# A ring of its own for the modulation weights, and another start: x first, constants off SyncE, first pieces of 2, 2, 4 and 8 row chunks

## The chip, the cores and the metric

The kernel runs on one core of one Trainium2 chip. The metric is the device time of one execution in microseconds (us). The engines named here are TensorE (PE; its weight loads are PEld), VectorE (DVE), ScalarE (ACT), GpSimd (POOL) and SyncE (SP), which in this kernel issues the loads of the large weights. PEclk is the share of full speed that TensorE's clock was granted.

## What is computed

One step of a transformer of two layers, width 2048, for 128 prompt tokens and 128 sample tokens. The two sets are called groups here. Each group has a conditioning vector (`c_ctx` for the prompt, `c` for the sample), from which every layer makes six vectors of 2048 (the modulation: shift1, scale1, gate1, shift2, scale2, gate2):

```python
mod_ctx = silu_ctx @ w_mod[l] + b_mod[l]
mod_lat = (silu_c @ w_mod[l] + b_mod[l])[:, None, :]
h = rmsnorm(x, norm1) * (1.0 + scale1) + shift1
proj = h @ w_in
mix = jnp.concatenate([attn_out, o_gla], axis=-1) @ w_out
x = x + gate1 * mix
h2 = rmsnorm(x, norm2) * (1.0 + scale2) + shift2
x = x + gate2 * (jnp.square(jax.nn.relu(h2 @ w_up)) @ w_down)
```

Between `proj` and `mix` stand softmax attention (8 heads, 2 of keys and values) and a gated linear attention (GLA) in two directions. All weights are float32. `w_mod` has 2048 x 12288 entries a layer, 201 MB for both layers; in all 613 MB are moved.

## The kernel before

**Products.** Each large product is cut into blocks of 512 output columns (`block`, L303). A block goes over its 2048 rows in chunks of 256 rows: SyncE loads a chunk (tile `raw`, 512 KB, L320, in a ring of eight buffers), ScalarE casts it (L107, `wh`) and VectorE subtracts (L108, `wl`), so that the weights stand in a high and a low part. The normed and transposed x stands in a high and a low part as well (`TH`, `TL`). For each chunk, group and half, TensorE makes three products: L345 (xh wh), L346 (xl wh) and L347 (xh wl). These are called products below; there are 8640 of them, counted from 1 in the order in which TensorE runs them. In layer 0, 1 to 432 are the first half of the rows of the input projection (nine blocks), 433 to 864 the second half, 865 to 1248 the output projection, 1249 to 4320 the MLP. Layer 1 has 4321 to 5184 (input projection), 5185 to 5568 (output projection), and the MLP.

**Modulation.** `w_mod` is loaded in tiles of 512 KB (`rawm`), as a rule 128 rows by 1024 columns. On TensorE (`mod_pe`, L210 to L224) a tile gives two float32 products of 32 rows by 512 columns (L219; the trace has two records for each) into a quarter of the tile `mod`; L195 and L197 then turn the sums. `mod_first` (L226 to L254) does the same for shift1 and scale1 of layer 0, in four quarters of their columns (L237), 16 tiles each. Some segments are summed on VectorE beside the MLP instead (`mod_dve`, L264 and L270). The modulation on TensorE is a generator that the blocks pump: `N_MOD` (L34) says how many tiles go with a block of each phase, `BATCH` that they go in fours, and `need` pumps until a named segment is done. The tiles come from the same ring as the weight chunks:

```python
raw = rawp.tile([P, 1024], F32, tag="raw", name="rawm")
nc.sync.dma_start(raw, I["w_mod"][l, kc * P:(kc + 1) * P, c0:c0 + 1024])
```

**Start.** SyncE loads the identity (L91), the conditioning vectors (L133, L134), rows of biases and norm weights (L153 to L158), and the first modulation tiles (L233); GpSimd loads x. x is normed without the modulation and transposed (`xT0`, L104). When a quarter of shift1 and scale1 is there, `modulate` makes the quarter of TH and TL, and after each of the first two quarters the nine blocks of the projection run over these two chunks. The sums wait in tiles `part`.

**Norms.** At a norm the second group lags behind the first by `LAG` chunks (L41). The first group's rows go over VectorE (`xn`, L368) to TensorE's transposes (`xnT`, L104), ScalarE and VectorE (`xv`, L379 and L381) to TH and TL.

**What sets the order.** The order on each engine is made by the tile framework with a simulated timeline, and each engine then runs its instructions in that order. A load stands in SyncE's queue until its buffer is free, and every load behind it waits as well.

## Time and profile before

| | |
|---|---|
| time of three executions | 2413.31, 2416.92, 2418.26 us (median 2416.92) |
| the profiled execution: span | 2416.7 us |
| TensorE busy | 2352.2 us, 97% |
| VectorE, ScalarE, GpSimd busy | 1635.4, 1090.3, 192.0 us |
| moved by DMA | 613.20 MB, 254 GB/s in the mean |
| granted TensorE clock, mean | 0.990 |

The first instruction and the last bound the span; the median of the times is 0.2 us longer. A busy time is the sum of an engine's instructions without overlap. In a list of waits the time is that in which the engine stood still in front of an instruction, put down to what came last. In a timeline each row is one or more like instructions in a row, with the time from the first start to the last end.

### The profile page before, as it was taken

The numbers are of one execution on the slowest core, as the hardware profiler recorded it, in microseconds if no ns is written. First come the engines' busy times: TensorE is split into PE (matmuls) and PEld (weight loads), VectorE is DVE, ScalarE is ACT, GpSimd is POOL, SyncE is SP. The second block draws the span as 40 slices with busy tenths as digits, with TensorE's granted clock in tenths as the row PEclk, the third lists the DMA queues.
The fourth block names the chain that finished last, engine by engine and source line by source line (L and its number), as shares of the span: only waits on it lengthen the run. The fifth ranks groups of instructions, "written<-read, shape, count | busy, mean of one in ns | idle before, by whom it ended". The sixth has DMA issues, their size and how long they took to land.

```text
span 2416.7 us, 32872 instructions
## 1 busy us (share of the span) xinstructions
PE 2352.2 (97%) x12533; PEld 1778.1 (74%) x12533; DVE 1635.4 (68%) x1936; ACT 1090.3 (45%) x1470; POOL 192.0 (8%) x253
## 2 busy tenths in 40 slices
PE   6999999989999999999999999999999999999998
PEld 2655555767878878878876767777788888888887
...
GB/s 299 270 335 332 288 277 281 284 290 191 297 301 310 303 278 309 296 184 296 302 273 256 184 233 230 245 263 263 227 287 279 190 177 202 189 183 191 193 179 182
DMA packets 274334, 613.20 MB, mean 254 GB/s; under 512 B 24273, under 2 KB 24785, under 8 KB 274177
## 3 DMA queue, kind: packets, MB, share of 16 engines
...
HBM read 601.01 MB, written 10.03 MB: 253 GB/s over the span
## 4 chain that ended last, share of the span: by engine, by line
PE 86%; DVE 4%; DMA 4%; issue 3%; POOL 1%; ACT 1%; SPq 0%; POOLq 0%; DVEq 0%; ACTq 0%
PE acc L345 25%; PE acc L347 25%; PE acc L346 25%; PE mod L219 4%; PE mod L237 2%; DVE wl L108 1%; DMA rawm<-in_w_mod_dram 1%; DMA raw<-in_w_up_dram 1%; PE aT L104 1%; DMA raw<-in_w_down_dram 1%; DVE ga L270 1%; DMA rows<-in_b_mod_dram 1%; PE sc L577 1%; PE mod L277 1%; PE xnT L104 1%
## 5 line engine op out<-in xcount | busy, mean ns | idle before, releaser
L108 DVE TENSOR_TENSOR wl<-raw,wh 128x1024 fp32r<-128x1024 f32 (+1 forms) x586 | 692.1, 1189 | 423.6 <-ACT wh L107 407.4
L107 ACT CAST wh<-raw 128x1024 fp32r<-128x1024 f32 (+1 forms) x586 | 592.4, 1017 | 785.1 <-PE acc L346 623.8
L345 PE MATMUL acc<-wh,TH 128*128 128x512 f32 x2248 | 892.8, 398 | 1.1 <-ACT wh L107 1.0
L346 PE MATMUL acc<-wh,TL 128*128 128x512 f32 x2248 | 882.5, 393 | 0.4 <-DVE TL L108 0.4
L347 PE MATMUL acc<-wl,TH 128*128 128x512 f32 x2248 | 862.4, 396 | 1.6 <-DVE wl L108 1.6
L345 PEld LDWEIGHTS acc<-wh,TH 128*128 128x128 f32 x2248 | 423.7, 189 | 139.5 <-issue 27.3
L347 PEld LDWEIGHTS acc<-wl,TH 128*128 128x128 f32 x2248 | 422.8, 189 | 126.4 <-issue 16.6
L346 PEld LDWEIGHTS acc<-wh,TL 128*128 128x128 f32 x2248 | 423.9, 189 | 94.0 <-issue 6.8
L270 DVE SCALAR_TENSOR_TENSOR ga<-rawm,CT,ga 128x1024 f32<-128x1024 f32 x300 | 378.1, 1278 | 28.8 <-DMA rawm<-in_w_mod_dram 27.7
L108 DVE TENSOR_TENSOR wx<-raw,wx 128x1024 fp32r<-128x1024 f32 (+1 forms) x182 | 194.5, 1079 | 102.8 <-ACT wx L107 102.7
L107 ACT CAST wx<-raw 128x1024 fp32r<-128x1024 f32 (+1 forms) x182 | 168.0, 937 | 192.6 <-PE acc L346 146.2
L345 PE MATMUL acc<-wx,TH 128*128 128x512 f32 x632 | 247.6, 392 | 0.0
L346 PE MATMUL acc<-wx,TL 128*128 128x512 f32 x632 | 246.9, 391 | 0.0
L347 PE MATMUL acc<-wx,TH 128*128 128x512 f32 x632 | 239.6, 390 | 0.0
L345 PEld LDWEIGHTS acc<-wx,TH 128*128 128x128 f32 x632 | 119.5, 189 | 25.9 <-issue 0.8
L346 PEld LDWEIGHTS acc<-wx,TL 128*128 128x128 f32 x632 | 119.4, 189 | 25.1
L347 PEld LDWEIGHTS acc<-wx,TH 128*128 128x128 f32 x632 | 119.2, 189 | 25.1
L219 PE MATMUL mod<-rawm,CT 128*32 128x512 f32 x640 | 115.8, 610 | 4.4 <-DMA rawm<-in_w_mod_dram 2.5
L237 PE MATMUL mod<-rawm,CT 128*32 128x512 f32 x256 | 58.2, 653 | 18.9 <-DMA rawm<-in_w_mod_dram 18.9
...
L219 PEld LDWEIGHTS mod<-rawm,CT 128*32 128x32 f32 x640 | 18.9, 109 | 45.0 <-issue 40.0
L812 ACT ACTIVATE relu<-acc 128x512 f32<-128x512 f32 x64 | 37.9, 592 | 30.4 <-PE acc L347 30.4
(242 smaller groups left out, 1343.2 us busy)
## 6 DMA issues: line engine op xcount, KB each, us to landing
...
raw<-in_w_up_dram SPq DMA_DIRECT2D x256, 512.0 KB, 4.6
raw<-in_w_down_dram SPq DMA_DIRECT2D x256, 512.0 KB, 5.3
...
```

Of the source, the lines that this page charges most:

```text
L104: nc.tensor.transpose(dst[:, j], s, ident)
L107: nc.scalar.copy(hi, v)
L108: nc.vector.tensor_tensor(out=lo, in0=v, in1=hi.bitcast(F32), op=ALU.subtract)
L219: nc.tensor.matmul(ps[32 * q:32 * q + 32, :], CT[:, 2 * kc:2 * kc + 32], raw[:, cc * 512:(cc + 1) * 512], start=kc == 0, stop=kc == KC - 1)
L237: nc.tensor.matmul(ps[r:r + 32, :], CT[:, 4 * ch + 2 * k:4 * ch + 2 * k + 32], raw[:, k], start=ch == 0, stop=ch == KC // 2 - 1)
L270: nc.vector.scalar_tensor_tensor(out=ga[g], in0=raw, scalar=c, in1=ga[g], op0=ALU.mult, op1=ALU.add)
L277: nc.tensor.matmul(ps[32 * q:32 * q + 32, :], unit[:, 1 - g:33 - g], acc[q // 2][g][:, (q % 2) * 512:(q % 2) * 512 + 512], start=g == 0, s ...
L345: nc.tensor.matmul(acc[g], xh, wh[:, k, :], start=first, stop=False)
L346: nc.tensor.matmul(acc[g], xl, wh[:, k, :], start=False, stop=False)
L347: nc.tensor.matmul(acc[g], xh, wl[:, k, :], start=False, stop=final)
L577: nc.tensor.matmul(sps[hh][w_ * c:w_ * c + w_, n], EB[r, n % 4, j0:j0 + w_], EA[r, n % 4, i0:i0 + w_], start=True, stop=True, tile_positio ...
L812: nc.scalar.activation(r, acc, AF.Relu)
```

## The change

- The modulation tiles on TensorE no longer come from the ring of the weight chunks, but by `mod_raw` from a ring that `in_turn` sets: in the first phase four slices of a buffer of tag TH and the tiles QT, KT, BF and BB; from each layer's start on eight slices of a TH and a TL buffer; from the second half of the Q columns on the ring of the weight chunks again (`shared`); and before the output projection eight slices of a TH and a TL buffer.
- x is loaded first, on SyncE; the identity and the conditioning vectors on ScalarE's queue; the rows of biases and norm weights on GpSimd's.
- shift1 and scale1 come in pieces of 2, 2, 4, 4 and 4 row chunks of 128 columns each (`FIRST`, then 8 to 12 and 12 to 16). The first two have tiles of 128 x 4 x 256 in place of 128 x 2 x 512. The nine blocks of the first phase run three times, over 1, 1 and 2 chunks of 256 rows, where they ran twice over 2.
- `N_MOD` has other numbers, and two of them a phase for the projections; the second norm's segments are asked for in the last block of the output projection and not before it.

```diff
-N_MOD = dict(a=(2, 4), b=9.25, out0=4, c=6, out1=3)
...
+N_MOD = dict(a=(0.9, 1.8, 3.6), b=(9, 5), out0=7.75, c=(7, 4), out1=4)
+FIRST = ((0, 2), (2, 4), (4, 8))
...
-        nc.sync.dma_start(ident, I["ident"])
+        nc.scalar.dma_start(ident, I["ident"])
...
+        rowt = big("PM", (P, 8, P), "rowt")
...
+        nc.scalar.dma_start(crow[0:16], I["c_ctx"].rearrange("(k p) -> k p", p=P))
+        nc.scalar.dma_start(crow[16:32], I["c"].rearrange("o (k p) -> (o k) p", p=P))
+        x0 = []
+        for g, n in enumerate(("x_prompt", "x_sample")):
+            x0.append([big("E", name="x0") for _ in range(2)])
+            for h in range(2):
+                nc.sync.dma_start(x0[g][h], I[n][0][:, h * 1024:(h + 1) * 1024])
...
-            nc.sync.dma_start(rows[0:96], I["b_mod"][l].rearrange("(k p) -> k p", p=P))
-            nc.sync.dma_start(rows[96:112], I["norm1"][l].rearrange("(k p) -> k p", p=P))
...
+            load(rows[0:96], I["b_mod"][l].rearrange("(k p) -> k p", p=P))
+            load(rows[96:112], I["norm1"][l].rearrange("(k p) -> k p", p=P))
...
-        def mod_turn(ps):
+        def mod_turn(ps, n=4):
...
-            for h in range(2):
+            for h in range(n // 2):
...
+        ring, turn = [], [0]
+        def in_turn(*parts):
+            ring[:] = [p for ps in zip(*parts) for p in ps] if len(parts) > 1 else parts[0]
+            turn[0] = 0
+        def bank(tag):
+            t = tp.tile([P, 4, 1024], F32, tag=tag, name="bank")
+            return [lambda j=j: t[:, j] for j in range(4)]
+        def mod_raw():
+            make = ring[turn[0] % len(ring)]
+            turn[0] += 1
+            return make()
+        shared = [lambda: rawp.tile([P, 1024], F32, tag="raw", name="rawm")]
...
                 for half in range(2):
-                    raw = rawp.tile([P, 1024], F32, tag="raw", name="rawm")
+                    raw = mod_raw()
...
-        def mod_first(l, q):
+        def mod_first(l, k0, nk):
             ps = ps_mod.tile([P, 512], F32, tag="mod", name="mod")
-            for ch in range(KC // 2):
+            n, per = nk * P, 8 // nk
+            for ch in range(KC // per):
                 for a in range(2):
-                    raw = rawp.tile([P, 2, 512], F32, tag="raw", name="rawm")
-                    c0 = a * D + q * 512
-                    nc.sync.dma_start(raw, I["w_mod"][l, ch * 256:(ch + 1) * 256, c0:c0 + 512]
+                    raw = mod_raw().rearrange("p (c n) -> p c n", n=n)
+                    c0 = a * D + k0 * P
+                    nc.sync.dma_start(raw, I["w_mod"][l, ch * per * P:(ch + 1) * per * P, c0:c0 + n]
                                       .rearrange("(c p) n -> p c n", p=P))
-                    for k in range(2):
-                        r = 32 * (a * 2 + k)
-                        nc.tensor.matmul(ps[r:r + 32, :], CT[:, 4 * ch + 2 * k:4 * ch + 2 * k + 32], raw[:, k],
-                                         start=ch == 0, stop=ch == KC // 2 - 1)
-                    if ch < KC // 2 - 1 or a < 1:
+                    for k in range(per):
+                        kc = ch * per + k
+                        r = 32 * (a * 2 + k % 2)
+                        nc.tensor.matmul(ps[r:r + 32, 0:n], CT[:, 2 * kc:2 * kc + 32], raw[:, k],
+                                         start=kc < 2, stop=kc >= KC - 2)
+                    if ch < KC // per - 1 or a < 1:
                         yield
-            pt = mod_turn(ps)
...
-        on_pe = mods([(mod_first, 0, q) for q in range(4)]
+        on_pe = mods([(mod_first, 0, k0, k1 - k0) for k0, k1 in FIRST + ((8, 12), (12, 16))]
...
-            tiles = [big("E", name="x0") for _ in range(2)]
-            for h in range(2):
-                load(tiles[h], x_in[g][:, h * 1024:(h + 1) * 1024])
             ss = stile(4, "ss")
-            xt = [tiles[q // 2][:, (q % 2) * 512:(q % 2) * 512 + 512] for q in range(4)]
+            xt = [x0[g][q // 2][:, (q % 2) * 512:(q % 2) * 512 + 512] for q in range(4)]
...
+        in_turn(bank("TH"), [lambda t=t: big(t, name="rawm") for t in ("QT", "KT", "BF", "BB")])
...
-        for q in range(4):
-            need(0, "first", q)
+        def first(k0, k1):
+            need(0, "first", k0)
             for g in range(2):
-                modulate(0, 0, g, q, xT0[:, 4 * q:4 * q + 4, g * P:(g + 1) * P], TH, TL)
-            if q > 1:
-                continue
+                modulate(0, 0, g, k0, k1 - k0, xT0[:, k0:k1, g * P:(g + 1) * P], TH, TL)
+        for i, (k0, k1) in enumerate(FIRST):
+            first(k0, k1)
...
-                block(TH, TL, I["w_in"][0][:, c0:c0 + 512], None, keep, N_MOD["a"][q], [2 * q, 2 * q + 1])
+                block(TH, TL, I["w_in"][0][:, c0:c0 + 512], None, keep, N_MOD["a"][i], list(range(k0 // 2, k1 // 2)))
+        for k0 in (8, 12):
+            first(k0, k0 + 4)
...
+            in_turn(bank("TH"), bank("TL"))
...
+            mod_rate = [N_MOD["bc"[l]][0]]
...
-                    block(TH, TL, w_in[:, c0:c0 + 512], at, fin, N_MOD["c"], None, side)
+                    block(TH, TL, w_in[:, c0:c0 + 512], at, fin, mod_rate[0], None, side)
...
-                    block(TH, TL, w_in[:, c0:c0 + 512], None, fin, N_MOD["b"], [4, 5, 6, 7], side)
+                    block(TH, TL, w_in[:, c0:c0 + 512], None, fin, mod_rate[0], [4, 5, 6, 7], side)
...
             QA[0] = proj(Q_A, q_a, side=lv[2:4])
+            in_turn(shared)
+            mod_rate[0] = N_MOD["bc"[l]][1]
             QA[1] = proj(Q_A + 512, q_a, side=[att(0, 0), lv[4], att(1, 0), lv[5]])
...
             x1 = [[big(t, name="x1") for t in ts_] for ts_ in (("QT", "KT"), ("BF", "BB"))]
             ss1 = [stile(4, "ss1") for g in range(2)]
+            in_turn(bank("TH"), bank("TL"))
             H2 = new_t()
 
...
             for n in range(NB):
-                for s in (2,) if n < NB - 1 else (4, 3):
-                    need(l, s)
+                need(l, 2)
...
                     if n == NB - 1:
+                        need(l, 4)
+                        need(l, 3)
                         norm(l, 1, g, [piece(x1[g], q) for q in range(4)], ss1[g], *H2)
```

The order of the instructions changes in all phases. First, SyncE at the start. Before, from the fourth row on (ahead of it stand the identity and the conditioning vectors; `rawm` are modulation tiles, an x3 means three in a row):

```order
L233 DMA rawm<-in_w_mod_dram 128x2x512 x3
L153 DMA rows<-in_b_mod_dram 96x128
L154 DMA rows<-in_norm_dram 16x128
L155 DMA rows<-in_norm_dram 16x128
L157 DMA grow<-in_b_gate_fwd_dram 4x128
L158 DMA grow<-in_b_gate_bwd_dram 4x128
L153 DMA rows<-in_b_mod_dram 96x128
L154 DMA rows<-in_norm_dram 16x128
L155 DMA rows<-in_norm_dram 16x128
L157 DMA grow<-in_b_gate_fwd_dram 4x128
L158 DMA grow<-in_b_gate_bwd_dram 4x128
L233 DMA rawm<-in_w_mod_dram 128x2x512 x13
```

After, from the third row on (`x_110` and `x_111` are the last two of the four tiles of x; `bank` and `rawm` the modulation tiles; `raw` weight chunks):

```order
L142 DMA x_110<-in_x_sample_dram 128x1024
L142 DMA x_111<-in_x_sample_dram 128x1024
L260 DMA bank<-in_w_mod_dram 128x4x256
L260 DMA rawm<-in_w_mod_dram 128x4x256
L260 DMA bank<-in_w_mod_dram 128x4x256
L260 DMA rawm<-in_w_mod_dram 128x4x256
L260 DMA bank<-in_w_mod_dram 128x4x256
L260 DMA rawm<-in_w_mod_dram 128x4x256
L260 DMA bank<-in_w_mod_dram 128x4x256
L260 DMA rawm<-in_w_mod_dram 128x4x256
L348 DMA raw<-in_w_in_dram 128x2x512 x8
```

Four tiles of x and eight of modulation stand ahead of the first weight chunks, where sixteen tiles of modulation and thirteen small loads stood.

Second, TensorE at the transposes of K (`kaT`) in layer 0's projections. Before:

```order
L345 MATMUL acc_2044<-wh,TH 128x512
L346 MATMUL acc_2044<-wh,TL 128x512
L347 MATMUL acc_2044<-wl,TH 128x512
L638 MATMUL kaT<-ident,part 128x128 x2
L219 MATMUL mod<-rawm,CT 32x512 x8
L345 MATMUL acc_2043<-wh,TH 128x512
```

After:

```order
L374 MATMUL acc_2051<-wh,TL 128x512
L375 MATMUL acc_2051<-wl,TH 128x512
L611 MATMUL sc<-EA,EB 64x64 x32
L245 MATMUL mod<-bank,CT 32x512 x6
L672 MATMUL kaT<-ident,part 128x128 x2
L373 MATMUL acc_2051<-wh,TH 128x512
```

Six modulation products stand ahead of the transposes, and eight stood behind them.

Third, TensorE in layer 0's output projection, behind the last product of a projection that uses the old TH (`po` and `PT` belong to the attention, `ksT` to the linear one). Before, at the place where modulation next runs after product 870:

```order
L345 MATMUL acc_3688<-wh,TH 128x512
L346 MATMUL acc_3688<-wh,TL 128x512
L347 MATMUL acc_3688<-wl,TH 128x512
L219 MATMUL mod<-rawm,CT 32x512 x4
L345 MATMUL acc_3687<-wh,TH 128x512
L346 MATMUL acc_3687<-wh,TL 128x512
L347 MATMUL acc_3687<-wl,TH 128x512
L345 MATMUL acc_3687<-wh,TH 128x512
L219 MATMUL mod<-rawm,CT 32x512 x2
L346 MATMUL acc_3687<-wh,TL 128x512
```

After, at product 890:

```order
L375 MATMUL acc_3591<-wl,TH 128x512
L245 MATMUL mod<-bank,CT 32x512 x4
L106 MATMUL PT<-ident,PM 128x128 x4
L205 MATMUL mod<-ident,modt 128x128 x2
L709 MATMUL po<-PTs,cv 128x512
L106 MATMUL PT<-ident,PM 128x128 x4
L205 MATMUL mod<-ident,modt 128x128 x2
L245 MATMUL mod<-bank,CT 32x512 x10
L709 MATMUL po<-PTs,part 128x512
L373 MATMUL acc_3591<-wx,TH 128x512
```

The runs of modulation products here are longer than before, and stand nearer to the products that read the buffers in which their tiles will lie. SyncE's loads for them, after, from the first chunks of w_out on:

```order
L348 DMA raw<-in_w_out_dram 128x2x512 x9
L242 DMA bank<-in_w_mod_dram 128x1024 x8
L348 DMA raw<-in_w_out_dram 128x2x512 x3
L242 DMA bank<-in_w_mod_dram 128x1024 x2
L348 DMA raw<-in_w_out_dram 128x2x512
L242 DMA bank<-in_w_mod_dram 128x1024 x6
L348 DMA raw<-in_w_out_dram 128x2x512 x2
L242 DMA bank<-in_w_mod_dram 128x1024 x4
L348 DMA raw<-in_w_out_dram 128x2x512
L242 DMA bank<-in_w_mod_dram 128x1024 x14
L348 DMA raw<-in_w_out_dram 128x2x512 x16
```

In the order before, the loads of this stretch alternate too, but each of them waits for a buffer of the ring of weight chunks only.

## Rows read from the trace of the kernel before

**Rows 1.** The page's first part: busy time of each engine, its share of the span, and its instructions.

```profile
PE 2352.2 (97%) x12533; PEld 1778.1 (74%) x12533; DVE 1635.4 (68%) x1936; ACT 1090.3 (45%) x1470; POOL 192.0 (8%) x253
```

**Rows 2.** TensorE's waits over the whole execution: the waiting instruction, what it waited for, us in total, times, longest.

```profile
PE mod L237 <- DMA rawm<-in_w_mod_dram: 18.9, 9, 5.4
PE xnT L104 <- DVE xn L368: 10.1, 5, 6.5
```

**Rows 3.** The start in windows of 5 us: length, busy time of each engine, then PEclk, the share of time that the DMA engines were busy, and GB/s.

```profile
0.00:5.00 5.00, 0.28 (x1) 0.18 (x1) 0.54 (x6) 1.51 (x2) 3.93 (x11) 1.00 0.43 104
...
15.00:20.00 5.00, 1.01 (x4) 0.19 (x4) 0.00 (x0) 0.00 (x0) 0.00 (x0) 1.00 0.46 110
...
45.00:50.00 5.00, 1.40 (x4) 0.22 (x4) 4.70 (x13) 4.29 (x8) 0.00 (x0) 0.50 1.05 388
50.00:55.00 5.00, 5.00 (x13) 2.00 (x12) 0.81 (x2) 0.01 (x1) 0.00 (x0) 0.57 1.05 385
```

**Rows 4.** SyncE's waits in the first 60 us, as in rows 2.

```profile
SPq L155 <- DMA rawm<-in_w_mod_dram: 7.0, 1, 7.0
...
SPq L154 <- DMA rawm<-in_w_mod_dram: 3.7, 1, 3.7
```

**Rows 5.** TensorE's timeline at the start: start, us, instruction, and in brackets the idle time before it. L237 is a modulation tile, L345 the first product.

```profile
41.74 1.05 PE L237 MATMUL mod<-rawm,CT 128*32 128x512 f32 x4 [1.75 <-DMA rawm<-in_w_mod_dram]
...
50.46 1.65 PE L345 MATMUL acc<-wh,TH 128*128 128x512 f32 x3
...
53.88 0.70 PE L346 MATMUL acc<-wh,TL 128*128 128x512 f32 x1
```

**Rows 6.** TensorE's timeline around three runs of modulation products (x4: one tile, x8: two, x12: three).

```profile
200.29 0.40 PE L347 MATMUL acc<-wl,TH 128*128 128x512 f32 x1
200.62 1.05 PE L219 MATMUL mod<-rawm,CT 128*32 128x512 f32 x4
201.60 0.50 PE L345 MATMUL acc<-wh,TH 128*128 128x512 f32 x1
...
202.86 0.39 PE L347 MATMUL acc<-wl,TH 128*128 128x512 f32 x1
203.17 1.07 PE L219 MATMUL mod<-rawm,CT 128*32 128x512 f32 x8
204.17 0.50 PE L345 MATMUL acc<-wh,TH 128*128 128x512 f32 x1
...
211.05 1.91 PE L219 MATMUL mod<-rawm,CT 128*32 128x512 f32 x12
```

**Rows 7.** The instructions on the tile `mod` alone, by stage: length of the stage, busy time of PE, PEld and DVE, then PEclk, DMA share and GB/s of the stage.

```profile
60.00:198.00 138.00, 40.62 (x212) 7.52 (x212) 4.23 (x18) 1.00 0.90 308
198.00:420.00 222.00, 66.70 (x336) 11.13 (x336) 2.19 (x8) 0.98 0.83 290
420.00:548.00 128.00, 12.19 (x68) 2.34 (x68) 1.08 (x4) 0.96 0.86 286
1291.00:1596.00 305.00, 35.04 (x222) 6.40 (x215) 1.09 (x4) 0.99 0.72 233
1596.00:1700.00 104.00, 1.83 (x12) 0.71 (x12) 1.09 (x4) 0.98 0.74 242
```

**Rows 8.** TensorE at the transposes of K and of Q in layer 0: two rows of the timeline, and the two windows of 10 us around them (columns as in rows 3).

```profile
275.15 0.50 PE L638 MATMUL kaT<-ident,part 128*128 128x128 f32 x2 [3.72 <-DVE part L613]
...
314.28 1.11 PE L104 MATMUL qaT<-ident,part 128*128 128x128 f32 x4 [2.21 <-DVE part L625]
...
270.00:280.00 10.00, 6.27 (x29) 2.79 (x28) 9.81 (x16) 5.66 (x10) 4.53 (x5) 0.83 0.41 141
310.00:320.00 10.00, 7.79 (x162) 6.01 (x162) 9.08 (x11) 3.09 (x11) 6.84 (x6) 0.83 0.70 222
```

**Rows 9.** TensorE's timeline at layer 0's second norm, from the output projection's last product to the MLP's first, and the window behind it.

```profile
535.85 0.39 PE L347 MATMUL acc<-wx,TH 128*128 128x512 f32 x1
542.71 1.12 PE L104 MATMUL xnT<-ident,xn 128*128 128x128 f32 x4 [6.47 <-DVE xn L368]
544.73 1.11 PE L104 MATMUL xnT<-ident,xn 128*128 128x128 f32 x4 [0.90 <-DVE xn L368]
546.83 1.09 PE L104 MATMUL xnT<-ident,xn 128*128 128x128 f32 x4 [0.99 <-ACT xv L379]
547.57 0.78 PE L345 MATMUL acc<-wh,TH 128*128 128x512 f32 x1
...
547.60:553.00 5.40, 5.40 (x17) 4.21 (x16) 2.60 (x6) 3.09 (x7) 0.00 (x0) 0.53 0.00 0
```

**Rows 10.** TensorE's timeline at layer 1's first norm (modulation tiles inside it), and at its second.

```profile
1290.05 1.92 PE L219 MATMUL mod<-rawm,CT 128*32 128x512 f32 x14
...
1293.26 1.05 PE L219 MATMUL mod<-rawm,CT 128*32 128x512 f32 x4 [0.70 <-DMA rawm<-in_w_mod_dram]
1296.11 1.05 PE L219 MATMUL mod<-rawm,CT 128*32 128x512 f32 x4 [1.80 <-DMA rawm<-in_w_mod_dram]
...
1683.53 0.63 PE L104 MATMUL xnT<-ident,xn 128*128 128x128 f32 x4 [1.28 <-DVE xn L368]
```

**Rows 11.** Two windows of the first phase: length, busy time of PE, PEld, DVE, ACT and POOL, PEclk, DMA share, GB/s.

```profile
60.00:120.00 60.00, 60.00 (x273) 36.86 (x271) 23.81 (x30) 28.25 (x39) 0.00 (x0) 1.00 0.83 268
...
60.00:198.00 138.00, 136.95 (x618) 79.94 (x617) 63.20 (x90) 51.74 (x69) 0.58 (x1) 1.00 0.90 308
```

55 lines of the change are left out of this document (27 added, 28 removed).

## The prediction

> **What bounds the kernel now.** I read the busy shares first, then what TensorE waited for, then the slices of the start, then TensorE's timeline around each stall, then the modulation's time by stage. TensorE is busy for 2352.2 of 2416.7 us [rows 1], so only 64.5 us are idle, and the reader is to see in [rows 2] that its waits are few and named: 18.9 us for modulation tiles, 10.1 us for normed rows. The change keeps every product of the 8,640 for the projections and the MLP, so the time moves only by (a) when the first product starts, (b) what TensorE spends on modulation products after that, and (c) waits that go or come. The end of the kernel is TensorE's end; each of these adds or takes its full length.
>
> The profiled execution spans 2416.7 us, 0.2 us under the median of the three times (2416.92). My sum is made against the span.
>
> **The start.** DMA runs at 388 GB/s when it is fed [rows 3], so a 512 KB tile takes 524,288 / 388,000 = 1.35 us. Between 15 and 20 us it moves 110 GB/s: SyncE holds two small row loads for 3.7 and 7.0 us [rows 4], and everything behind them in its queue stands. The last modulation product of the first piece starts at 41.74, the first product at 50.46, and they run without a break only from 53.88 [rows 5], with a granted clock of 0.50 and 0.57 in these slices, which is the 1.2 GHz level for most of the time [rows 3]. After the change, twelve tiles (four of x, eight of modulation) stand in front of the first piece's end instead of sixteen tiles and the rows: about 5 us until data flow (the first slice moves 104 GB/s) plus 12 x 1.35 = 21 us. The way from the last modulation product to the first product (50.46 - 41.74 = 8.7 us, and 3.4 us more to 53.88) leads through VectorE and ScalarE, and is longer now: the order puts 28 transposes of x and two tiles of the second piece ahead of the first product. I take 21 + 1 + 8.7 and 8.7 once more for that = 39.4, so the unbroken run starts 14.5 us earlier. Ends: -19 (half of the second 8.7 hidden) and -8 (the x chain alone sets it, first run at 46).
>
> The row loads move to other queues. [Rows 3, 4] show the 16 DMA engines half idle at 0.46 while SyncE waited. The Trainium skill (DMA: Bandwidth & Descriptors, "Issuing engines are not separate DMA queues") says that DMAs of all issuers run on the same 16 engines, and that several issuers save only the time to issue. By that rule alone only the eight tiles would be saved, 8 x 1.35 = 10.8 us; the trace speaks for more, since the engines it names had room.
>
> **Modulation products.** [Rows 6] give the price of one uninterrupted run between products: from the product before it to the one after it 1.31 us with one tile (x4 records are two matmuls), 1.31 us with two tiles; two products alone are 0.23 apart, and the next product is 0.1 longer. So a run of one or two tiles costs 1.16 us, and each further pair 0.85 to 0.97 (three tiles: 1.91 in place of 1.07). I counted runs in both orders and priced them so:
> - products 1 to 432 (first phase): 34 runs, 43.3 us before; 32 runs, 42.9 after, -0.4
> - 432 to 864 (other half of layer 0's projections): 54 runs of 164 matmuls, 70.4 us before; 41 of 134, 57.3 after, -13.1
> - 864 to 1248 (its output projection): 10 runs of 32, 12.6 before; 18 of 68, 26.7 after, +14.1
> - from 1248 on: 27 runs of 116, 40.1 before; 38 of 128, 53.8 after, +13.7. Twelve more matmuls, and many runs of a single tile where it had runs of four.
>
> Sum +14.3, with ends +10 and +18. As a test, busy time on the tile `mod` by stage in [rows 7] is 40.62, 66.70, 12.19 and 36.87, near the prices of before without the switches.
>
> The switch itself (0.2 us in a run) is dear here because of the runs' number. The Trainium skill (TensorEngine Tiling (Array Packing), "Key Properties") says that a change of the tiling mode drains TensorE. The rows agree, since a run starts 0.31 to 0.33 after the product before it, and the product behind it lasts 0.50 [rows 6]. By that rule alone, with 132 runs before and 134 after, the change costs 2 x 0.2 us and no more; what I charge comes from half-filled runs.
>
> **Waits that go.** (1) In layer 0's attention TensorE sat 3.72 us before the transposes of K and 2.21 us before those of Q, and the granted clock of these 10 us slices fell to 0.83, which costs 1.7 us each [rows 8]. The order now puts 3 tiles (6 matmuls) ahead of the one and 5 ahead of the other. They are priced above, so the waits and the clock go: -9.3 with all of them (5.9 + 3.4); ends 0 and -9.3. Their cover is the tiles being there in time. (2) Layer 0's second norm: idle 6.47 + 0.90 + 0.99 us, and the next 5.4 us at a clock of 0.53, 2.5 us lost [rows 9]. The second group's last stretch is now 36 products long and was 21, and the last transposes of the norm's modulation stand 22 products ahead of its end: 15 x 0.23 = 3.4 us at least, 10.9 at most; I take -6.5, because layer 1's second norm, which nothing interrupts, still keeps an idle step of 1.28 us [rows 10]. (3) Layer 1's first norm had fifteen modulation matmuls in it, some of which waited 0.70 and 1.80 us for DMA [rows 10]; their work is counted above, and without it the norm's own steps come out: +1 (ends -3, +4).
>
> **Waits that come.** (1) The last of the five pieces (row chunks 12 to 16 of 128) ends inside the block Q_G, and its way to TH, 8.7 us as at the start, is covered by 11 products and a run, about 3.7; half the rest was the slow clock: +3.5 (0 to 5). (2) Thirty matmuls of modulation stand around the Q transposes, with loads from the shared ring behind them: +2 (0 to 5). (3) Before the output projection the ring lies in the TH and TL that the last projection products read. 34 tiles cannot be loaded until then, and in SyncE's queue w_out's loads stand among them: 41 tiles in all until the last early run. At 1.35 us that is 55 us; TensorE's work to there is about 60, an estimate: 110 products at 0.23 are 25, 33 tiles some 22 at the prices above, and I put 13 for some 80 small matmuls. In total covered, in its middle not: +6. Ends 0, and +15 if the tiles come at the 286 GB/s of that stage [rows 7], 1.83 us each and 75 in all. (4) Layer 1's second norm starts 20 products before the end where it had 35: 15 x 0.23 = +3.4 (0 to 6).
>
> **Sum.** -14.5 + 14.3 - 9.3 - 6.5 + 1 + 3.5 + 2 + 6 + 3.4 = -0.1, so 2416.7 - 0.1 + 0.2 = 2416.8, no change. VectorE's additions and ScalarE's copies for nine more blocks lie beside products: VectorE is busy 63.20 of 138 us there [rows 11].
>
> **The rivals.**
> - Faster: the ring does what rings do, and none of the four new waits shows. For it: with a clear start TensorE was 60.00 of 60 us busy in the first phase [rows 11]. Against it: the order loads bank tiles only after the products that read them. 2416.8 - 14.9 = 2402.
> - Slower: the bank tiles come late. In the output projection of layer 0 they come at 1.83 us, 75 us of loading against 60 us of work, +15 for my +6; and at layer 1's start, where the ring lies in tiles that the last MLP products read, the first products wait another 5 us like the tiles in [rows 10] (0.70 and 1.80, now with eight in a row). 2416.8 + 9 + 5 = 2431. It decides from 1.5 us a tile on (41 x 1.5 = 61, TensorE's work). For it: 0.86 of the DMA time was taken in that stage already [rows 7]. Against it: fed alone, the loads came at 1.35 [rows 3].
> - The start does not do what it says: the x chain on ScalarE and VectorE sets the first product, the run begins at 46 and not at 39.4: 2416.8 + 6.6 = 2423.
>
> **How the numbers follow.** Chances: the forecast 0.42 (2416.8, with 2409 to 2425 as its own range from the ends of the middle terms), faster 0.28, slower 0.20, late start 0.10. What a measurement of this kernel can tell from no change is 0.2%, 4.8 us, so the bounds are 2412.1 and 2421.8. Faster: 0.28 and 0.10 of the forecast's lower edge, 0.38. Same: 0.23 of the forecast and 0.04 of the late start, 0.27. Slower: 0.20, 0.06, and 0.09 of the forecast's upper edge, 0.35. The range reaches just past both of the outer cases, 2400 to 2432.
>
> **What would show it.** Step by step: the first unbroken products begin near 39 us; TensorE's time on `mod` rises by about 14 us between the output projection and layer 1 and falls by 13 in the second half of layer 0's projections; the lines on K's and Q's transposes leave the list of waits; `mod` from the bank tiles appears in it between products 894 and 974, with DMA as releaser; the gap before layer 0's MLP is near 5 us. I am wrong if the time from 864 to 1248 does not grow by 13 us or so, if layer 1's projections grow by under 8, or if the products start after 46.

## The result and the profile after

The changed kernel takes 2429.30 us (median of six runs, 2425.75 to 2436.39), the kernel before beside it 2417.18 (six runs, 2413.31 to 2422.14). The ratio is 1.0051 [1.0037, 1.0065]: slower by half a per cent, where no change (2416.8) was forecast. The time lies in the range, near the price of the slower rival, but that rival's mechanism is not what happened.

The profiled execution spans 2426.9 us, 10.3 more than before (2416.66 to 2426.94). First part of the changed kernel's page:

```profile
PE 2359.4 (97%) x12597; PEld 1784.9 (74%) x12597; DVE 1642.3 (68%) x1961; ACT 1091.2 (45%) x1472; POOL 191.1 (8%) x259
```

Against [rows 1] TensorE is busy 7.2 us longer, and its idle time went from 64.5 (2416.7 - 2352.2) to 67.5 us. Its waits over the changed kernel's whole execution:

```profile
PE xnT L106 <- DVE xn L396: 10.9, 6, 4.4
PE cps L144 <- DMA rowt<-in_c_dram: 7.1, 1, 7.1
PE xnT L106 <- DVE xT L436: 5.8, 3, 4.4
PE mod L265 <- DMA rawm<-in_w_mod_dram: 4.5, 2, 4.1
PE mod L245 <- DMA bank<-in_w_mod_dram: 4.4, 5, 2.4
PE mod L265 <- DVE t L121: 4.3, 1, 4.3
PE kaT L672 <- DVE y L659: 4.2, 1, 4.2
...
PE mod L265 <- issue: 2.3, 1, 2.3
```

The 18.9 us of [rows 2] for first-piece tiles are gone, and smaller waits stand in their place, most of them at the start too. The line on K's transposes is layer 1's, not layer 0's as in [rows 8].

**Where the time went.** I counted the products in both traces and took their starts from the timeline. A difference is after less before. The last column says how many of TensorE's 224 modulation tiles of 512 KB had started by then, before and after:

| | before | after | difference | tiles |
|---|---|---|---|---|
| product 1 | 50.46 | 43.24 | -7.2 | 17, 10 |
| product 217 (middle of the first half) | 120.36 | 119.89 | -0.5 | 38, 38 |
| product 433 (second half of the rows) | 197.97 | 188.94 | -9.0 | 68, 59 |
| product 1249 (layer 0's MLP) | 547.57 | 533.92 | -13.7 | 166, 160 |
| product 4320 (last of that MLP) | 1289.73 | 1272.66 | -17.1 | 166.5, 160 |
| product 4421 (100 behind layer 1's first norm) | 1329.49 | 1319.89 | -9.6 | 178, 174 |
| product 5568 (last of layer 1's output projection) | 1680.81 | 1687.39 | +6.6 | 224, 224 |
| product 5569 (layer 1's MLP) | 1685.58 | 1694.48 | +8.9 | 224, 224 |
| end | 2416.7 | 2426.9 | +10.3 | 224, 224 |

Layer 0 came out 17 us ahead, but not all of that is a gain: six tiles that it did before, at about 1 us each (a lone one takes 1.05 in [rows 6]), are left to layer 1. From layer 1's first norm to the end 27.4 us were lost, and nearly all before its MLP.

**The start.** TensorE's timeline of the changed kernel, which answers to [rows 5]:

```profile
33.56 1.11 PE L106 MATMUL xnT<-ident,xn 128*128 128x128 f32 x4 [4.43 <-DVE xT L436]
...
39.33 1.92 PE L265 MATMUL mod<-bank,CT 128*32 128x256 f32 x8
...
43.24 0.48 PE L373 MATMUL acc<-wh,TH 128*128 128x512 f32 x1
...
44.81 1.06 PE L265 MATMUL mod<-bank,CT 128*32 128x256 f32 x8
45.80 0.66 PE L106 MATMUL xnT<-ident,xn 128*128 128x128 f32 x4
```

The first product starts at 43.24, and second-piece tiles and x's transposes stand between the next ones. The lead is 7.2 us at product 1, where seven tiles fewer have been done, and 0.5 at product 217, where both kernels have done 38: what had filled the start of before now stands among the products. At product 433 the lead is 9.0 us again, with nine tiles fewer. Windows of 5 us of the changed kernel (columns as in [rows 3]):

```profile
15.00:20.00 5.00, 1.58 (x12) 0.37 (x4) 0.00 (x0) 0.00 (x0) 0.00 (x0) 1.00 0.97 226
...
30.00:35.00 5.00, 1.11 (x4) 0.71 (x4) 3.71 (x6) 3.71 (x9) 0.00 (x0) 0.61 1.05 383
35.00:40.00 5.00, 3.96 (x17) 2.70 (x19) 4.23 (x14) 1.33 (x5) 0.00 (x0) 0.50 1.09 353
```

From 15 to 20 us the DMA engines are now 0.97 busy and move 226 GB/s, where [rows 3] had 0.46 and 110. The lower of the clock's two levels (1.2 GHz, a granted 0.50) is still there, at 30 to 40 us.

**The modulation by stage**, the instructions on the tile `mod` as in [rows 7]. Changed kernel, windows cut to whole us at the products above (and near 865, 5185 and 5568, which bound the projections):

```profile
0.00:43.00 43.00, 14.45 (x82) 5.18 (x82) 0.98 (x5) 0.88 1.01 325
43.00:189.00 146.00, 40.40 (x230) 8.98 (x230) 3.76 (x17) 1.00 0.90 309
189.00:386.00 197.00, 53.59 (x276) 9.49 (x276) 2.50 (x10) 1.00 0.79 272
386.00:529.00 143.00, 31.45 (x144) 5.67 (x144) 2.21 (x8) 0.98 0.89 307
...
1281.00:1582.00 301.00, 36.37 (x196) 6.38 (x196) 1.09 (x4) 0.98 0.65 210
1582.00:1688.00 106.00, 13.86 (x68) 2.74 (x68) 1.10 (x4) 1.00 0.84 297
...
sum 2420.00, PE 209.30 PEld 43.73 DVE 17.09; mean PE 26.16 PEld 5.47 DVE 2.14
```

The kernel before, where [rows 7] have no row with these cuts, and below them the stretch of layer 1's first norm:

```profile
0.00:50.00 50.00, 20.56 (x72) 3.04 (x72) 1.40 (x6) 0.94 0.90 307
50.00:198.00 148.00, 43.07 (x218) 7.70 (x216) 4.23 (x18) 0.99 0.89 306
...
1290.00:1591.00 301.00, 35.99 (x226) 6.75 (x226) 1.09 (x4) 0.99 0.72 231
...
sum 2410.00, PE 200.56 PEld 37.10 DVE 16.49; mean PE 25.07 PEld 4.64 DVE 2.06
...
1290.00:1300.30 10.30, 6.08 (x30) 0.98 (x30) 0.00 (x0) 1.00 0.98 339
```

Second half of the rows: 53.59 for 66.70, -13.1. Layer 0's output projection: 31.45 for 12.19, +19.3. Layer 1's is 13.86 where [rows 7] have 1.83, +12.0. Its input projection looks unchanged (36.37 for 35.99), but 6.08 us of the latter lay inside the norm, in time that TensorE would otherwise have stood idle.

**The norms and K.** Timeline of the changed kernel around layer 0's second norm, layer 1's first, layer 1's K transposes, and layer 1's second norm:

```profile
528.88 0.39 PE L375 MATMUL acc<-wx,TH 128*128 128x512 f32 x1
529.61 0.63 PE L106 MATMUL xnT<-ident,xn 128*128 128x128 f32 x4 [0.34 <-DVE xn L396]
...
533.92 0.77 PE L373 MATMUL acc<-wh,TH 128*128 128x512 f32 x1
...
1277.43 1.08 PE L106 MATMUL xnT<-ident,xn 128*128 128x128 f32 x4 [4.38 <-DVE xn L396]
1279.42 1.12 PE L106 MATMUL xnT<-ident,xn 128*128 128x128 f32 x4 [0.90 <-DVE xn L396]
1281.10 0.80 PE L373 MATMUL acc<-wh,TH 128*128 128x512 f32 x1 [0.57 <-ACT TH L109]
...
1392.45 0.59 PE L672 MATMUL kaT<-ident,y 128*128 128x128 f32 x2 [0.58 <-DVE y L647]
1392.97 0.79 PE L611 MATMUL sc<-EA,EB 64*32 64x32 f32 x68
1397.99 0.66 PE L672 MATMUL kaT<-ident,y 128*128 128x128 f32 x2 [4.23 <-DVE y L659]
...
1690.82 1.08 PE L106 MATMUL xnT<-ident,xn 128*128 128x128 f32 x4 [3.04 <-DVE xn L396]
```

Layer 0's second norm takes 533.92 - 528.88 = 5.0 us where [rows 9] show 547.57 - 535.85 = 11.7. Layer 1's first norm has no modulation left in it and stands idle for 4.38 + 0.90 + 0.57. Between the K transposes of its two groups lie only the small `sc` products, so TensorE waits for the second group's way over VectorE and GpSimd, 4.23 us. The second norm of layer 1 waits 3.04 us where the row of [rows 10] waited 1.28. What the idle time does to the clock, in windows of 10 us of the changed kernel:

```profile
1271.00:1281.00 10.00, 4.25 (x18) 2.78 (x16) 7.48 (x19) 4.09 (x11) 0.74 (x2) 0.80 0.94 299
1281.00:1291.00 10.00, 9.90 (x36) 6.76 (x40) 5.04 (x15) 4.68 (x13) 0.00 (x0) 0.69 1.01 398
...
1395.00:1405.00 10.00, 7.01 (x77) 5.51 (x78) 2.90 (x4) 2.38 (x6) 4.43 (x6) 0.66 0.54 157
...
1690.00:1700.00 10.00, 7.69 (x23) 5.95 (x24) 6.03 (x14) 5.12 (x11) 0.61 (x1) 0.50 0.39 148
```

and of the kernel before, at layer 1's first norm:

```profile
1290.00:1300.00 10.00, 7.49 (x43) 2.24 (x42) 6.36 (x14) 3.60 (x8) 0.54 (x1) 1.00 0.98 338
1300.00:1310.00 10.00, 10.00 (x50) 7.77 (x52) 6.53 (x17) 5.39 (x13) 0.00 (x0) 1.00 0.92 347
```

Before, the norm ran at full clock (2.4 GHz) throughout. In the changed kernel 0.69 over 9.9 busy us behind the norm costs about 3 us, and 0.66 over the 7 around the second K transposes about 2.4. From product 4320 to 4421 both kernels have the same modulation time (9.30 before, 9.12 after). The 7.5 us that this stretch grew by are idle time, 5.85 for 2.52 us, and the low clock, about 4.1 for none (busy time times the missing share of the clock, in windows of 1 us).

### The profile page after: what moved, and what is told of

It is laid out like the page before. It is cut to its first block, busy times and chain, and to the rows that moved or that the text cites. A ratio compares the mean times of both kernels' runs of the same rounds, so it can differ in the third digit from the quotient of the medians.

```text
span 2426.9 us, 33039 instructions
## 1 busy us (share of the span) xinstructions
PE 2359.4 (97%) x12597; PEld 1784.9 (74%) x12597; DVE 1642.3 (68%) x1961; ACT 1091.2 (45%) x1472; POOL 191.1 (8%) x259
## 4 chain that ended last, share of the span: by engine, by line
PE 88%; DVE 4%; DMA 3%; issue 2%; ACT 1%; POOL 1%; SPq 1%; POOLq 0%; DVEq 0%; ACTq 0%
PE acc L373 26%; PE acc L375 25%; PE acc L374 25%; PE mod L245 4%; PE mod L265 2%; DMA bank<-in_w_mod_dram 1%; PE aT L106 1%; DVE wl L110 1%; DMA rawm<-in_w_mod_dram 1%; PE xnT L106 1%; PE sc L611 1%; DVE ga L298 1%; DMA raw<-in_w_in_dram 1%; PE mod L305 1%; SPq L260 0%
## 5 line engine op out<-in xcount | busy, mean ns | idle before, releaser
L298 DVE SCALAR_TENSOR_TENSOR ga<-rawm,CT,ga 128x1024 f32<-128x1024 f32 x300 | 378.8, 1282 | 29.1 <-DMA rawm<-in_w_mod_dram 28.5
L110 DVE TENSOR_TENSOR wx<-raw,wx 128x1024 fp32r<-128x1024 f32 (+1 forms) x182 | 195.2, 1082 | 85.8 <-ACT wx L109 85.1
L245 PE MATMUL mod<-bank,CT 128*32 128x512 f32 x460 | 91.9, 618 | 4.9 <-DMA bank<-in_w_mod_dram 4.4
L106 PE MATMUL xnT<-ident,xn 128*128 128x128 f32 x128 | 25.0, 330 | 21.7 <-DVE xn L396 10.9
```

The source lines that it names most:

```text
L106: nc.tensor.transpose(dst[:, j], s, ident)
L110: nc.vector.tensor_tensor(out=lo, in0=v, in1=hi.bitcast(F32), op=ALU.subtract)
L245: nc.tensor.matmul(ps[32 * q:32 * q + 32, :], CT[:, 2 * kc:2 * kc + 32], raw[:, cc * 512:(cc + 1) * 512], start=kc == 0, stop=kc == KC - 1)
L298: nc.vector.scalar_tensor_tensor(out=ga[g], in0=raw, scalar=c, in1=ga[g], op0=ALU.mult, op1=ALU.add)
```

## The experiments

My theory when the experiments began: the loss is layer 1's, from the new ring, counts and needs. The rivals: tiles that come late from DMA, and a start that does less than it could. All runs, each with the kernel before on the same chip. Median and ratio are of all executions; the last five columns come from the profiled one alone, by the count of products as above. In them a few us can be chance: layer 0's MLP (1249 to 4320), whose products no run changes, takes 735.7 to 742.6 us. The columns: start of products 433 and 1249, time from product 4320 to 4421 (layer 1's first norm and 100 products), from 4421 to 5568, and from 5568 to 5569 (its second norm).

| run | median | ratio | 433 | 1249 | 4320-4421 | 4421-5568 | norm |
|---|---|---|---|---|---|---|---|
| before | 2417.2 | | 198.0 | 547.6 | 39.8 | 351.3 | 4.8 |
| after | 2429.3 | 1.0051 [1.0037, 1.0065] | 188.9 | 533.9 | 47.2 | 367.5 | 7.1 |
| e1, layer 1 as before | 2419.1 | 1.0003 [0.9992, 1.0014] | 189.3 | 535.3 | 43.7 | 363.3 | 5.1 |
| e2, layer 1 shared ring | 2423.3 | 1.0026 [1.0013, 1.0038] | 188.8 | 536.7 | 41.1 | 369.8 | 6.6 |
| e3, layer 1 old counts | 2416.6 | 0.9998 [0.9989, 1.0007] | 188.7 | 532.4 | 47.1 | 359.3 | 5.1 |
| e12, layer 1 old needs | 2428.5 | 1.0042 [1.0029, 1.0056] | 190.5 | 534.1 | 45.9 | 364.6 | 6.6 |
| e13, six and six | 2414.0 | 0.9993 [0.9983, 1.0004] | 188.7 | 534.4 | 46.6 | 358.5 | 5.1 |
| d1, seven and seven | 2417.2 | 1.0002 [0.9993, 1.0011] | 191.5 | 537.5 | 46.3 | 358.6 | 5.1 |
| e5, loads as before | 2433.8 | 1.0068 [1.0055, 1.0081] | 192.4 | 537.8 | 47.9 | 366.8 | 6.6 |
| e6, sums first | 2426.9 | 1.0043 [1.0029, 1.0057] | 190.4 | 534.9 | 47.1 | 367.4 | 7.1 |
| e9, row transposes apart | 2438.9 | 1.0092 [1.0078, 1.0105] | 191.9 | 545.4 | 48.2 | 366.8 | 6.6 |
| e11, e9 + e6 + small loads on SyncE | 2429.1 | 1.0053 [1.0040, 1.0066] | 180.6 | 535.1 | 47.6 | 366.6 | 6.6 |
| e4, old pieces | 2416.8 | 1.0003 [0.9994, 1.0012] | 195.2 | 537.2 | 48.8 | 356.0 | 5.1 |
| d2, six-six and nine-nine | 2413.2 | 0.9985 [0.9977, 0.9994] | 189.1 | 531.6 | 47.8 | 354.8 | 5.2 |
| f1, ring alone | 2412.6 | 0.9987 [0.9977, 0.9997] | 197.3 | 535.4 | 47.8 | 351.4 | 5.1 |
| f2, start alone | 2410.9 | 0.9985 [0.9975, 0.9996] | 192.0 | 535.0 | 41.5 | 357.9 | 5.1 |
| f3, old pieces, d2's counts | 2408.2 | 0.9968 [0.9954, 0.9981] | 193.6 | 530.3 | 47.8 | 351.9 | 4.9 |
| g1, f3 + layer 1 shared ring | 2403.5 | 0.9945 [0.9931, 0.9958] | 196.1 | 532.6 | 40.1 | 352.8 | 5.1 |

### Layer 1 undone, whole and in parts

e1 puts layer 1's ring, counts and needs back; e2 the ring alone, e3 the counts and needs alone. The ring:

```diff
-            in_turn(bank("TH"), bank("TL"))
...
+            if l == 0:
+                in_turn(bank("TH"), bank("TL"))
+            else:
+                in_turn(shared)
```

The counts and needs (the first line's other entries stay):

```diff
-N_MOD = dict(..., c=(7, 4), out1=4)
+N_MOD = dict(..., c=(6, 6), out1=3)
...
-                need(l, 2)
+                for s in (2,) if n < NB - 1 or l == 0 else (4, 3):
+                    need(l, s)
```

e1: 

> Layer 0 as in the changed kernel, layer 1 as before: modulation tiles from the ring of the weight chunks, 6 tiles a block in the projections, 3 in the output projection, the second norm's segments asked for before the last block. The changed kernel was 16.4 us ahead at product 1344 and 10.3 us behind at product 6000. Theory 1 (the loss is layer 1's ring and counts): nearly all of the 26.7 us come back, 2400 to 2405 us. Theory 2 (layer 1 pays for modulation products that layer 0 no longer does, 128 in place of 116, and the order prices them at 53.6 us here, 53.8 in the changed kernel, 40.1 before): little comes back, 2420 or more.

e2: 

> Only the ring of layer 1 is undone: its modulation tiles come from the ring of the weight chunks, with the new counts. Theory 1a (the banks come late, since the MLP's and the projections' last products read them): the first norm's gap is filled again with modulation products and the bunch behind it goes, about 10 us back, 2419 us; the out-projection's share too, 2410 to 2419. Theory 1b (the counts do it): no change, 2427 to 2430.

e3: 

> Only layer 1's counts are undone (6 a block, 3 in the output projection, the second norm's segments before the last block), with its ring of banks kept. Theory 1b (the counts): 10 to 18 us back, since the output projection of layer 1 grew by 18.3 us, 2411 to 2419. Theory 1a (late banks): no change or slower, 2427 to 2435.

e1 gives back 10 us, e2 alone 6, e3 alone 12 to 13. The parts don't add up, and none reaches layer 0's lead of 17. e1 falls short because its layer 1 still holds more modulation than before: layer 0 leaves it six tiles more (at product 1249 e1 has done 160 of the 224, as the changed kernel has), and from product 4421 to 5568 `mod` takes 42.8 us where the kernel before has 28.5. That is near its theory 2. e2's trace shows a gain in one place, layer 1's first norm (41.1 for 47.2), where the shared ring lets modulation products in again; its profiled execution (2429.1) was the slowest of its six. Its time lies between its two theories, e3's in the range of theory 1b. e3 gains in the stretch behind it (359.3 for 367.5) and at the second norm. To part counts from needs, e12 took the needs alone back, e13 one pair of numbers, and d1 another pair as a control:

```diff
-N_MOD = dict(..., c=(7, 4), out1=4)
+N_MOD = dict(..., c=(6, 6), out1=4)
```

e12: 

> Only one part of layer 1's counts is undone: its second norm's segments are asked for before the last block of the output projection, as before; 7 and 4 tiles a block stay. Theory 5a (asking inside the last block spreads the tiles to the end and delays the norm): the gap at product 5568 falls from 7.1 to under 5 us and 2 to 4 us come back, 2425 to 2427. Theory 5b (the counts 7 and 4 do it all): no change, 2428 to 2430.

e13: 

> Only the counts of layer 1's projections are undone, 6 and 6 tiles a block in place of 7 and 4; four in the output projection and the asking in its last block stay. Theory 5b: the wait of the transposes of K (4.8 us) goes, eight matmuls leave the output projection, and the whole gain of the old counts is here, 2415 to 2418. Theory 5a: less than half of it, 2422 to 2427.

d1 (c=(7, 7)): 

> Layer 1's counts go on in the direction of the six-and-six kernel: 7 and 7 tiles a block, so that no modulation product is left for the output projection (32 matmuls in the changed kernel, 24 with six and six). Theory 5b (each run in layer 1's output projection and the late end of its modulation is what cost): 3 to 5 us faster than with six and six, 2409 to 2412. Rival (the gain of six and six was the wait of the transposes of K alone): 2414 or more.

The needs cost nothing to speak of: e12's interval overlaps the changed kernel's, as theory 5b had it. The two numbers of e13 alone give back 15 us, just beyond the range of theory 5b. K's transposes and the second norm in e13's timeline:

```profile
1389.85 0.44 PE L672 MATMUL kaT<-ident,y 128*128 128x128 f32 x2
...
1397.99 0.44 PE L672 MATMUL kaT<-ident,y 128*128 128x128 f32 x2 [1.17 <-DVE y L659]
...
1676.14 0.63 PE L106 MATMUL xnT<-ident,xn 128*128 128x128 f32 x4 [0.42 <-DVE xn L396]
```

Products stand between the two K transposes again, and the wait is 1.17 us. Of `mod`, e13 leaves 7.99 us in the output projection where the changed kernel has 13.86:

```profile
1578.00:1676.00 98.00, 7.99 (x52) 1.74 (x52) 1.08 (x4) 1.00 0.88 300
```

The norm then waits 0.42 where it waited 3.04. d1 keeps the wait at K (4.23 us again) and leaves only 0.76 us of `mod` in the output projection; it still gives back 12 us. Its time is the one that its rival named, but not for the rival's reason, since K's wait stayed. What the runs move in layer 1 can be read from the stretch from product 4421 to 5568, cut into the time on `mod`, the idle time, the time lost to the low clock (as above) and the rest:

| run | 4421-5568 | `mod` | idle | clock | rest |
|---|---|---|---|---|---|
| before | 351.3 | 28.5 | 2.5 | 1.7 | 318.6 |
| after | 367.5 | 41.1 | 5.3 | 2.7 | 318.4 |
| e1 | 363.3 | 42.8 | 1.4 | 0.0 | 319.0 |
| e13 | 358.5 | 38.0 | 1.9 | 0.0 | 318.6 |
| d1 | 358.6 | 34.5 | 5.2 | 2.1 | 316.8 |
| e4 | 356.0 | 36.9 | 2.2 | 0.0 | 316.8 |
| f2 | 357.9 | 35.5 | 4.2 | 0.0 | 318.2 |

In all eighteen traces the rest lies between 316.8 and 319.2 us. So two causes move this stretch: the modulation in it, and the wait at K with the clock behind it. Against the kernel before, the modulation is the larger (12.6 of 16.2 us). Of e13's 9.0 us, 3.1 are modulation and 6.1 the idle time and the clock; of d1's 8.9, 6.6 are modulation.

### The start

e5 puts the loads on their queues of before, e6 computes both groups' row sums first, e9 takes the row transposes `cpt` out of the two PSUM buffers that x's transposes use, e11 is e9 and e6 with the small loads (`hn`, `cv`, `rope`) on SyncE:

```diff
-            cpt = mtile((P, 136), "cpt")
+            cpt = gtile((P, 136), "cpt")
```

e5: 

> The changed kernel with the loads at the start undone: identity, conditioning vectors and rows on SyncE, x on GpSimd; pieces and rings stay. Theory 7a (the move of the small loads off SyncE gives the 3.7 and 7.0 us that SyncE waited): first product 5 to 10 us later than 43.2, 2432 to 2438 if it arrives at the end, by theory 6b 2427 to 2432. Theory 7b (moved to GpSimd's queue the rows land later and hold back x's transposes, so that the move costs): first product earlier than 43.2.

e6: 

> The start alone is changed: the sums of squares of both groups of x stand ahead of both groups' transposes in the code, which in ScalarE's order puts the second group's four sums ahead of the first three casts of w_in (they stood behind, and ScalarE stood 16.8 us waiting for the first chunk). Theory 3 (ScalarE's queue holds the x chain and so the first product, at 43.2): first product near 37, 4 to 6 us gained at product 432 and at the end, 2423 to 2425. Rival (the first product waits for the modulation tiles, whose last one landed at 26.5, and for VectorE): first product within 1 us of 43.2, 2428 to 2430.

e9: 

> The changed kernel with one edit: the transposed rows of biases (cpt, two tiles) lie in the PSUM ring of the attention's scores and not in the ring of two buffers from which the transposes of x take theirs. Theory 3a (the rows, which now land by GpSimd's queue and are transposed behind five modulation tiles, hold both PSUM buffers, so that the order puts all of x's transposes behind the last tile of the first piece): the transposes now stand between the tiles, the first product comes near 34 in place of 43.2, 7 to 9 us gained at product 432, 2419 to 2422 us. Rival (the start is bound by VectorE's and ScalarE's work on the casts): first product within 2 us of 43.2, 2427 to 2430.

e11: 

> As the kernel with cpt apart, and also: the sums of squares of both groups first, and layer 0's small loads for the heads (norm weights, cached values, rope tables) issued by SyncE behind the first eight weight chunks and not by GpSimd at 9 to 12 us. Theory 4 (these small loads delay the modulation tiles, whose fourth took 14.6 us to land): the eighth tile lands near 21.5 in place of 26.5, first product near 29, 4 to 5 us more than with cpt apart alone, 2414 to 2417. Rival (the loads share the engines without cost to the tiles): the eighth tile within 1 us of 26.5 and the time of the kernel with cpt apart.

Product 1 starts at 33.85 in e5, 43.46 in e6, 34.37 in e9 and 32.12 in e11, for 43.24. So x's transposes were held back by the row transposes through the shared buffers (e5, e9), and not by ScalarE's order (e6, whose time lies between its two expectations). The rows' data were not what came late: on GpSimd's queue the last of them had landed at 14.17 us (21.10 before). It is TensorE's order that has the last three of the four row transposes at 24.91, 28.41 and 36.50 us, behind modulation tiles that land up to 26.51.

But no earlier start is a faster kernel: 9 us earlier at product 1, e5 and e9 are 4.5 and 9.6 us slower. e11 is 8 us ahead of the changed kernel at product 433, and 1.2 us behind at 1249. What the start leaves out of TensorE comes later, at a price that the pumping behind it sets: e5 and e9 have done eight tiles and not ten at product 1, and between products 1 and 865 `mod` takes 101.7 and 106.5 us for the changed kernel's 94.0. A later start is not a slower kernel either: product 1 comes at 55.59 in e4 and at 57.49 in f1 below. The times of e9 and e11 miss both their theories, although e9's first product came where theory 3a had it; e5's first product came earlier, as theory 7b had it. In e11 the small loads did delay the tiles, as theory 4 had it: the eighth lands at 22.00 us, in e9 at 25.98.

### The parts alone, and the best of them

```diff
-N_MOD = dict(a=(0.9, 1.8, 3.6), b=(9, 5), out0=7.75, c=(7, 4), out1=4)
-FIRST = ((0, 2), (2, 4), (4, 8))
+N_MOD = dict(a=(2, 4), b=(9, 9), out0=4, c=(6, 6), out1=4)
+FIRST = ((0, 4), (4, 8))
```

This is f3. e4 has only `a` and `FIRST` of it, d2 only `b`, `out0` and `c`. f1 leaves of the whole change nothing but the ring, f2 nothing but the start. g1 is f3 with layer 1's ring of e2.

e4: 

> The changed kernel with the first phase's pieces undone: 4 and 4 row chunks, then 8 to 12 and 12 to 16, two and four modulation tiles a block as before; loads and rings stay as changed. Theory 6a (what the start gains arrives at the end): sixteen tiles stand ahead of the first product again, 10.8 us later, so 2438 to 2441. Theory 6b (the second half of layer 0's projections gives a shift of the start back, as the two kernels did that started 9 and 11 us earlier and were not faster): 2426 to 2432.

d2: 

> Six and six in layer 1, and in layer 0 the same step: 9 and 9 tiles a block in the second half of the projections in place of 9 and 5, 4 in the output projection in place of 7.75, so that 32 matmuls and not 68 stand there and fewer tiles need the banks that come late. Theory 8a (the late banks and the crowded output projection of layer 0 cost: 4.9 us of waits for bank tiles there): 3 to 6 us faster than six and six alone, 2408 to 2411. Theory 8b (the price of the runs decides, 86.9 us in place of 84.0 in layer 0, 46.7 in place of 50.3 in layer 1): no difference, 2412 to 2416.

f1: 

> Only the ring of own buffers is left of the change: counts, needs, first pieces and loads are those of the kernel before. Theory that the ring matters (tiles no longer wait for one another, so norms and projections start earlier): below 2412, the waits of the K and Q transposes of the first layer gone and nothing new in the second layer. Rival, that buffers were never what the weights waited for and the gains in the first layer came from the counts: 2415 to 2419, with the waits at the first layer's K and Q transposes and its second norm about as before. Below 2412 or above 2420 would say that the ring has an effect of its own.

f2: 

> Only the new start is left of the change (loads, their queues, pieces of 2, 2, 4): the shared ring and the counts and needs of before follow it. Theory that the earlier first product is a gain: the start's milestone stays about 9 us ahead to the end, 2406 to 2410. Rival, that it removes no idle time of TensorE and the narrow pieces add about 7 us of modulation work: 2415 to 2425, with the lead at product 432 gone by product 1248 and 7 us more modulation work over the whole span.

f3: 

> First pieces of 4 and 4, six and six in the second layer's projections, nine and nine in the first layer's second phase and 4 in its output projection; ring and loads as changed. If the 7.6 us of narrow pieces and the 15 us of the counts are two separate costs: d2's 2413.2 less about 7, 2404 to 2408. If both edits undo one loss (the leftover of the second layer's modulation late in its output projection): 2411 to 2417.

g1: 

> The best variant so far (pieces of 4, six and six, nine and nine), with layer 1's modulation weights in the shared ring again. Theory that the ring in TH and TL empties layer 1's first norm of modulation products, and that the idle time and the low clock behind it cost about 6 us: from the last product before that norm to the hundredth behind it 41 us in place of 47.8, and 2402 to 2405 in all. Rival, that what the norm gains is lost again later in layer 1, because the shared ring's loads stand behind those of the projections (in e2 only part of the gain was left): 2406 to 2411, with the K transposes of layer 1 waiting again.

Alone, the ring and the start are each faster than before, by 0.13 and 0.15%; both intervals end below 1, but 0.2% is what the prediction took as the least that can be told from no change. Both times lie between their two expectations. What made the whole slower than either is above all layer 1's pair 7 and 4, and its price hangs on the pieces: 15.3 us with the narrow ones (after to e13), about 8.7 with the wide ones (e4 to f3, which differ in layer 0's counts too; these made 0.8 us between e13 and d2, as theory 8b had it). Both theories for e4 expected it slower than 2426, and it came at 2416.8. Wide pieces save 9.3 us of `mod` in e4 (199.97 in e4's row below, for the changed kernel's sum of 209.30) and 5.6 in f3 against d2 (195.17 for 200.81). A lone tile costs the same in either shape; what differs is how often tiles run alone or in pairs: between products 1 and 864 e4 has 62 runs of modulation, the changed kernel 73. e4's row:

```profile
0.00:2400.00 2400.00, 199.97 (x1032) 38.19 (x1032) 16.62 (x64) 0.99 0.77 255
```

f3 and g1 beat both kernels, g1 by 0.55% of before. f3's time was between its two expectations; e4's 12 us and e13's 15 are in part one loss: the wait at K falls in both, to 1.03 and 1.17 us, and the low clock behind it goes. g1's gain is where it was expected. Its windows at layer 1's first norm:

```profile
1266.00:1276.00 10.00, 9.88 (x53) 6.66 (x51) 9.18 (x20) 6.63 (x14) 0.54 (x1) 1.00 0.77 236
1276.00:1286.00 10.00, 8.43 (x38) 3.92 (x39) 7.80 (x17) 5.94 (x12) 0.54 (x1) 1.00 1.02 355
```

and the norm in its timeline:

```profile
1273.37 1.92 PE L245 MATMUL mod<-rawm,CT 128*32 128x512 f32 x16
...
1276.95 1.05 PE L245 MATMUL mod<-rawm,CT 128*32 128x512 f32 x4 [1.08 <-DMA rawm<-in_w_mod_dram]
1278.23 1.05 PE L245 MATMUL mod<-rawm,CT 128*32 128x512 f32 x4 [0.22 <-DMA rawm<-in_w_mod_dram]
```

Modulation fills the norm, the clock stays at 1.00, and the 101 products take 40.1 us for f3's 47.8, although two of the modulation tiles wait for DMA once more. Later it loses nothing.

## Why the prediction was wrong

By its stretches, against the traces: to product 433 it had -14.5 - 0.4 = -14.9, and -9.0 came; from there to layer 0's MLP -13.1 + 14.1 - 9.3 - 6.5 + 3.5 + 2 + 6 = -3.3, and -4.6 came; for that MLP nothing, and -3.4 came; from layer 1's first norm to the end +18.1, and +27.4 came. The miss is layer 1 (9.3 us) and the start (5.9); the stretches between came 4.7 us better than forecast.

- **Mis-sized: "Layer 1's first norm ... without it the norm's own steps come out: +1 (ends -3, +4)".** From product 4320 to 4421 the changed kernel takes 7.5 us longer with the same modulation time. Taking 6.08 us of modulation out of the norm shortened it only from 10.55 to 8.44 us (1300.28 - 1289.73 and 1281.10 - 1272.66), so +4.0, and the clock behind it cost about 3 more. The step priced the norm's modulation as work that moves; it had been nearly free where it stood. g1 shows it: put back alone, it is worth 7.7 us there and 4.6 between the medians. The prediction gave the reason for the emptiness (the ring lies in tiles that the last MLP products read) as part of a rival, for a DMA wait that didn't come.
- **Missing: K's transposes in layer 1.** The prediction read them in layer 0 alone. There the two waits went as forecast; in layer 1, under counts of 7 and 4, 4.81 us stand where 0.8 stood, and the clock costs 2.4. Since other waits of before went, the stretch from product 4421 to 5568 has about 3 us more idle time and 1 us more of low clock. In e13, with products between the two transposes again, 1.17 us are left.
- **Mis-sized: the start, -14.5.** The run that the term put at 39.4 began at 43.24, so -10.6 came against 53.88. The reason, which e5 and e9 show and the sum did not hold, is the row transposes in x's buffers; the rival of the late start named the x chain on ScalarE and VectorE. From there to product 433 the changed kernel then took 1.6 us more and not 0.4 less, with 2.3 us of idle time ahead of a modulation tile, for which the trace names no cause. And an earlier product 1 was no gain by itself: the three runs that brought it forward by 9 to 11 us did not get faster by it.
- **Right in sum, partly by luck: the modulation, +14.3.** From product 1 on, `mod` took 194.85 us (209.30 - 14.45) for 180.00 (200.56 - 20.56): +14.9. By place it was -2.7, -13.1, +19.3 and +11.4 in all that follows, for -0.4, -13.1, +14.1 and +13.7, so errors of 5 us cancel. The step on the drain gives 132 and 134 runs, where its own list adds up to 125 and 129; nothing hangs on it.
- **Right: layer 0's waits.** Its second norm had -6.5 and came out 6.7 shorter, with 1.3 us more from the clock behind it (0.80 over 6.10 us, for 0.53 over 5.40). For the bank tiles it had +6; five waits of 4.4 us came, at products 912 and 936, and the clock (0.87 and 0.79 from 406 to 426 us) cost about 3, part of it in the +19.3. Around the transposes of K and Q the waits went (3.72 and 2.21 us), but small ones came: from product 433 to 865 TensorE is idle for 4.6 us, 6.4 before. **Layer 1's second norm** had +3.4; 2.3 came at the norm and 1.4 behind it.
- **Nearly nothing came: the last piece's +3.5.** That piece ends at 201.8 us, behind product 457, and the one product that waits for its TH waits 0.76 us.

None of the signs that it had named for being wrong appeared: the time from product 865 to 1249 grew by 20.8 us, layer 1's projections (4321 to 5568) by 25.8, and the first product came before 46.

Of the rivals, the slower one had the right sign and nearly the time, by another way: bank tiles late by 15 us and first products of layer 1 waiting for DMA. Measured were 4.4 us of the first, none of the second.

What stays open: why wide first pieces give another order in layer 1. The 11.5 us that they save there (e4, 356.0 for 367.5) can be placed: 4.2 are `mod`, 3.1 idle time, 2.7 the clock, and 1.6 lie in the rest. So can f2's 357.9 us for 351.3 with counts and ring of before: `mod` takes 7 us more. But no run shows how the simulated timeline came to these orders, nor why seven and four leave K's transposes without products between them.
